# Differential attention on one Trainium2 core: half of the probability tiles take VectorE and DRAM instead of TensorE's transpose

## The chip, the cores and the metric

The kernel runs on one core of a Trainium2 chip. A core has TensorE (PE, matrix products and transposes through an identity), VectorE (DVE), ScalarE (ACT) and GpSimd (POOL), which run side by side and wait for each other through semaphores; here every DMA is issued from SyncE's queue (SP). The metric is device microseconds of one execution. The kernel before has a median of 1415.15 us over three runs (1411.51 to 1417.58); its profiled execution took 1413.83 us, of which 1412.0 us lie between the first and the last instruction (the span).

## The reference: what is computed

A trunk of two layers over 1024 tokens of width 1024. Each layer normalizes its input, modulates it by vectors made from a condition, runs an attention branch with a SiLU gate and adds the projected result to the residual. Layer 0 is differential attention: eight heads, each with two sets of 64-wide queries and keys and one 128-wide value.

```python
sc = einsum('bqhcd,bkhcd->bhcqk', qb, k) * scale      # c = 0, 1: two score maps a head
p = softmax(sc, axis=-1)
p = p[:, :, 0] - lam * p[:, :, 1]
o = einsum('bhqk,bkhd->bqhd', p, v)
o = rmsnorm(o, subln_g) * (1 - lambda_init)
o = o.reshape(b, s, DA_WIDTH) * silu(z)
```

Layer 1 is multi-head latent attention with one score map a head. The change lies in layer 0.

## The kernel before, in words

**Precision.** Operands are float32 numbers split into a high part, rounded to the format that TensorE multiplies, and a low remainder; each product is three matmuls, high by high, high by low and low by high (`mm3`, lines L203 to L205). A tensor that comes out of PSUM is thus copied on ACT (the high part) and subtracted on DVE or POOL (the low part).

**Layer 0's attention.** `attn0` (L1145) handles a head as four pairs of query tiles, `qp` 0 to 3, each of two tiles of 128 queries, `t` 0 and 1: eight slots a head, counted through all heads by `now[0]`. `q_tile` (L895) makes one tile: four matmuls for the score map c=0 into a PSUM buffer of 128x1024, a maximum on DVE (L433) and an exponential on ACT (L436) into an SBUF tile `e`; then the same for c=1, whose exponential stays in PSUM; a reciprocal and a scaling (L911, L912) and one DVE instruction (L913) that combines both into `e`. PSUM holds two score buffers, so map c=0 of a tile takes the buffer that the previous tile's c=0 left, and map c=1 takes the one that the previous tile's L913 has read last.

**The transpose.** P times V needs the tile with the keys on the partitions. `transpose_p` (L409) does half a tile, `kh` 0 or 1: four PE transposes of 128x128 into one PSUM buffer (L414), the high copy on ACT (L416), the low part on DVE (L419). A `Tail` (L1006) is a tile on this way: its first half is turned in the next slot, behind that slot's second score map, its second half one slot later, between that slot's two score maps. `settle` (L1093) puts the pair's products with V (`pv`, 24 matmuls with 256 columns) into the slot after the one that follows its second tile. The two pairs of a half head add into one PSUM buffer; when both are in, `close` reads it on ACT (`head_out`, L976 and L977), `subln` normalizes it with a small sum on PE in the next slot (`ssq`, L990), and `finish` (L942) spreads the row factors through DRAM, scales on POOL, splits, and stores to DRAM for the output projection.

**What fills TensorE between.** A second stream of work, the projections of the next heads (a strip for k, one for q, one for the gate, 16 steps each, a step being one `mm3` with 512 columns, product `acc`), is dealt out in steps between the pieces of a slot. `FILL0` (L41) says how many steps go into each of a slot's six places: behind score map 0, behind the second half-tile of the older tail, behind score map 1, behind the first half-tile of the newer tail, and behind each half of `pv`. Its sum over eight slots is 47. Each step also ticks a side queue, which runs the rest of a projected strip a few steps later: rotary embedding on POOL and DVE with a swap of partitions by DMA, then `stack_k` or `stack_q` (L372), which splits on ACT and POOL; `stack_q` then copies both parts to the other half of the partitions by DMA (`swap`, L384).

**The order of the instructions.** A planner orders the program at build time: on each engine it takes what its cost model finds ready, by priority in the order of the code. Three devices hold it: `pin` ties a PE instruction behind the PE instruction written before it, while `pinned[0]` is set; `behind(engine)` ties to the last marked instruction of an engine, held in `mk`; `in_turn` does for POOL what `pin` does for PE. In layer 0 `pinned[0]` is not set. In layer 1's attention it is.

**Layer 1 already has the other way.** There a pair with even `qp` is a `Mate` (L1037) and not two `Tail`s. `move` transposes the tile on DVE in blocks of 32x32 (L1047) into `eT` and stores it to DRAM (L1048). Two slots after the pair's second tile `fetch` loads both tiles from DRAM in four DMAs whose addressing moves the blocks to their place (L1054, tile `pr`). `high` (slot +4) makes the high parts on ACT (L1065), `low` (slot +5) the low parts on DVE (L1084), and the products with V come at slot +6. No PE transposes are left for that pair. The exponential that comes after `high` in the code is tied behind `high`'s copies on ACT.

Of the kernel before, what the change touches and what calls it, by code (L numbers as in the profile page):

```python
# [40 lines left out]
FILL0 = ((1, 2, 1, 1, 1, 0), (1, 1, 1, 1, 1, 1)) * 3 + ((1, 2, 1, 1, 1, 0), (1, 1, 1, 1, 1, 0))  # L41
# [57 lines left out]
def trunk(ctx: ExitStack, tc: tile.TileContext, A, out):  # L99
# [325 lines left out]
    def alloc_pt(ap_):  # L425
        pth = [ap_.tile([P, 4, 2 * P], F32R, name="pth", tag="pt", bufs=8 if ap_ is not a0b else 6) for _ in range(2)]
        ptl = [ap_.tile([P, 4, 2 * P], F32R, name="ptl", tag="pt", bufs=8 if ap_ is not a0b else 6) for _ in range(2)]
        return pth, ptl

    def softmax_part(ap_, s_ps, zs, bufs=3):  # L430

        nm = sm.tile([P, 1], F32, name="nm")
        mk["V"] = V.reduce_max(nm, s_ps, axis=AX.X, negate=True).ins  # L433
        e = ap_.tile([P, T], F32, name="e", tag="e", bufs=bufs) if ap_ else s_ps
        with tc.issue_after(mk.pop("H")) if "H" in mk else nullcontext():
            ex = S.activation(e, s_ps, AF.Exp, bias=nm, scale=1.0, accum_out=zs)  # L436
            pin_last(ex)
            mk["S"] = ex.ins
        return e
# [455 lines left out]
    def q_tile(h, half, ti, zz, ep, mid=lambda i: None):  # L895
# [5 lines left out]
        for c in range(2):  # L901
            s_ps = bank("sc", "s", [P, T])
            for src, fst in ((qa, True), (qb, False)):
                for kc in range(2):
                    PE.matmul(s_ps[:, kc * HF : (kc + 1) * HF], src[:, c, ql], KS[h][kc][:, c, :], start=fst, stop=not fst)  # L905
# [7 lines left out]
        combined.append(V.scalar_tensor_tensor(out=e0, in0=e1, scalar=z1[:, 0:1], in1=e0, op0=ALU.mult, op1=ALU.add).ins)  # L913
        return e0
# [27 lines left out]
    def finish(o, y, l, h, half, dst, ap_, dgs):  # L942

        if dst is None:
# [92 lines left out]
    class Mate(Tail):  # L1037
# [36 lines left out]
        def low(self, eng=V):  # L1074
# [18 lines left out]
    def settle(e, tail, mate, t, qp, ctx_, late):  # L1093
# [16 lines left out]
        elif t and not (late and qp == 3):  # L1110
            due.setdefault(n + (3 if late and qp == 0 else 2), []).extend([lambda: tail.pv(0), lambda: tail.pv(1)])
# [33 lines left out]
    def attn0(h, fills, extra=None, late=None):  # L1145
# [51 lines left out]

    for h in range(NH - 1):
        attn0(h, lambda i: FILL0[i])
    def load_ot(dst, src):  # L1200
# [943 lines left out]
```

## Time and profile before

| | |
|---|---|
| median of three runs | 1415.15 us |
| the profiled execution | 1413.83 us, its span 1412.0 us |
| PE busy | 1374.9 us, 97% of the span |
| DVE busy | 936.7 us, 66% |
| ACT busy | 740.3 us, 52% |
| POOL busy | 610.6 us, 43% |
| mean granted TensorE clock | 0.995 |
| DMA | 230.98 MB, 53.5% of 16 engines' span |

The times are those of a hardware profiler. PE's busy time counts a matmul from its start to its modelled end, and matmuls overlap; what one costs on a full PE is the distance between starts. Layer 0's attention runs from about 148 us (its first score map) to about 684 us (its last L913), layer 1's from 971 us to about 1317 us.

### The profile page before, as it was taken

What the parts mean: (1) busy time and instruction counts of PE and PEld (TensorE: products, weight loads), DVE (VectorE), ACT (ScalarE), POOL (GpSimd) and SP (SyncE); (2) the same over time, 40 slices, a digit from 0 to 9 for tenths busy, and PEclk for the clock granted to TensorE, in tenths of its full rate; (3) what the DMA queues carried; (4) which work ended last, traced back from release to release, by engine and by line L of the source; (5) the groups of instructions that cost most, each with busy time, mean ns of one, the idle gap of its engine ahead of it and who ended that gap; (6) DMA issues with size and microseconds to landing.
All of it is one profiled execution on the core that took longest, in us unless ns stands there. A gap on an engine that the chain in (4) does not pass through costs nothing.

```text
span 1412.0 us, 20440 instructions
## 1 busy us (share of the span) xinstructions
PE 1374.9 (97%) x7254; PEld 1150.0 (81%) x7254; DVE 936.7 (66%) x1365; ACT 740.3 (52%) x1290; POOL 610.6 (43%) x484
## 2 busy tenths in 40 slices
PE   9999899999999999999999999999999999998997
PEld 7778688888888888787778878888888888887886
DVE  7756687676777767678445787346777776764455
ACT  6623366666565655566443654345555555644342
POOL 4415164646564646462563235513142432313662
PEclk9999999999999999999999999999999999999999
DMA  9877723233333232336672222448688787776663
GB/s 352 262 226 233 237 66 103 79 103 83 105 85 95 80 96 81 97 87 221 219 240 97 97 90 90 126 146 261 164 223 248 213 240 195 204 214 214 226 213 129
DMA packets 147736, 230.98 MB, mean 164 GB/s; under 512 B 19121, under 2 KB 70449, under 8 KB 147634
## 3 DMA queue, kind: packets, MB, share of 16 engines
q1 hardware_dynamic: 147634, 229.68, 53.5%
q8 instruction: 57, 0.93, 0.3%
q14 instruction: 45, 0.37, 0.1%
HBM read 145.79 MB, written 60.23 MB: 146 GB/s over the span
## 4 chain that ended last, share of the span: by engine, by line
PE 78%; DMA 7%; DVE 6%; issue 3%; ACT 3%; SPq 2%; POOL 1%; ACTq 0%; POOLq 0%; DVEq 0%
PE acc L203 9%; PE acc L205 9%; PE acc L204 9%; PE s L1831 8%; PE s L905 7%; PE tr L414 6%; PE pv L204 4%; PE pv L205 4%; PE pv L203 4%; PE oacc L204 3%; PE oacc L205 3%; PE oacc L203 3%; PE zacc L203 1%; PE zacc L205 1%; PE zacc L204 1%
## 5 line engine op out<-in xcount | busy, mean ns | idle before, releaser
L433 DVE TENSOR_REDUCE nm<-s 128x1 f32<-128x1024 f32 x192 | 234.0, 1219 | 87.8 <-PE s L905 66.6
L416 ACT CAST pth<-tr 128x512 fp32r<-128x512 f32 x200 | 117.4, 587 | 212.8 <-PE tr L414 211.9
L436 ACT ACTIVATE e<-s,nm 128x1024 f32<-128x1024 f32 x128 | 143.2, 1119 | 94.6 <-DVE nm L433 94.2
L419 DVE TENSOR_TENSOR ptl<-tr,pth 128x512 fp32r<-128x512 f32 x200 | 137.2, 686 | 75.8 <-ACT pth L416 75.7
L254 POOL TENSOR_TENSOR wl<-wraw,wh 128x512 fp32r<-128x512 f32 (+2 forms) x82 | 102.7, 1254 | 170.4 <-ACT wh L253 162.8
L203 PE MATMUL acc<-h0h,wh 128*128 128x512 f32 x360 | 151.6, 421 | 1.8 <-DVE v_hl L393 1.7
L203 PE MATMUL pv<-pth,vt 128*128 128x256 f32 x512 | 146.4, 286 | 0.0
L204 PE MATMUL pv<-ptl,vt 128*128 128x256 f32 x512 | 145.2, 284 | 0.1
L205 PE MATMUL pv<-pth,vt 128*128 128x256 f32 x512 | 144.5, 282 | 0.0
L205 PE MATMUL acc<-h0h,wl 128*128 128x512 f32 x360 | 143.3, 398 | 0.1
L204 PE MATMUL acc<-h0l,wh 128*128 128x512 f32 x360 | 142.4, 396 | 0.0
L414 PE MATMUL tr<-ident,e 128*128 128x128 f32 x800 | 120.9, 273 | 10.1 <-DVE ptl L419 10.0
L414 PEld LDWEIGHTS tr<-ident,e 128*128 128x128 f32 x800 | 96.2, 140 | 41.6 <-DVE ptl L419 16.3
L1234 POOL TENSOR_TENSOR wol<-wor,woh 128x512 fp32r<-128x512 f32 x64 | 86.6, 1372 | 77.4 <-ACT woh L1233 71.4
L204 PEld LDWEIGHTS pv<-ptl,vt 128*128 128x128 f32 x512 | 97.2, 190 | 5.1 <-DVE ptl L419 0.4
L203 PEld LDWEIGHTS pv<-pth,vt 128*128 128x128 f32 x512 | 97.0, 189 | 4.5 <-ACT pth L416 0.4
L205 PEld LDWEIGHTS pv<-pth,vt 128*128 128x128 f32 x512 | 97.6, 191 | 0.1
L905 PE MATMUL s<-ks,qa 128*128 128x512 f32 x256 | 82.7, 403 | 6.0 <-ACT e L436 3.0
L913 DVE SCALAR_TENSOR_TENSOR e<-s,z,e 128x1024 f32<-128x1024 f32 x64 | 82.1, 1283 | 2.1
L355 POOL TENSOR_TENSOR rp_sw<-rp_sw,sinT 128x512 f32<-128x512 f32 x42 | 55.3, 1316 | 62.8 <-DMA rp_sw<-rp_raw 57.6
L205 PEld LDWEIGHTS acc<-h0h,wl 128*128 128x128 f32 x360 | 68.3, 190 | 16.4 <-POOL wl L254 0.6
L905 PE MATMUL s<-ks,qb 128*128 128x512 f32 x256 | 81.1, 396 | 0.0
(632 smaller groups left out, 3442.2 us busy)
## 6 DMA issues: line engine op xcount, KB each, us to landing
ada<-in_ada_ss SPq DMA_DIRECT2D x32, 512.0 KB, 6.4
wraw<-in_w_s SPq DMA_DIRECT2D x64, 256.0 KB, 2.8
vS<-v_hl SPq DMA_DIRECT2D x32, 512.0 KB, 5.0
vt<-vS SPq DMA_DIRECT2D x32, 512.0 KB, 5.0
wor<-in_w_out SPq DMA_DIRECT2D x64, 256.0 KB, 4.2
pS<-eT SPq DMA_DIRECT2D x28, 512.0 KB, 2.9
pr<-pS SPq DMA_DIRECT2D x56, 256.0 KB, 6.2
rp_sw<-rp_raw SPq DMA_DIRECT2D x168, 64.0 KB, 2.0
```

The costliest lines, as they stand in the source:

```text
L203: pin(PE.matmul(psum, ah, bh, start=first, stop=False))
L204: pin(PE.matmul(psum, ah, bl, start=False, stop=False))
L205: mm = PE.matmul(psum, al, bh, start=False, stop=last)
L254: sub = (lo_on or (V if pair_of else G)).tensor_sub(l_[:, :n], raw[:, :n], f32v(h_[:, :n]))
L414: pin(PE.transpose(tr[:, j, :], p[:, kt * P : (kt + 1) * P], ident))
L416: cp = S.copy(pth[kh][:, :, dst], tr)
L419: mk["V"] = V.tensor_sub(ptl[kh][:, :, dst], tr, f32v(pth[kh][:, :, dst])).ins
L433: mk["V"] = V.reduce_max(nm, s_ps, axis=AX.X, negate=True).ins
L436: ex = S.activation(e, s_ps, AF.Exp, bias=nm, scale=1.0, accum_out=zs)
L905: PE.matmul(s_ps[:, kc * HF : (kc + 1) * HF], src[:, c, ql], KS[h][kc][:, c, :], start=fst, stop=not fst)
L1234: in_turn(G.tensor_sub(lo, raw, f32v(hi)))
L1831: pin(PE.matmul(s_ps[:, kc * HF : (kc + 1) * HF], lhs, rhs(kc), start=i == 0, stop=i == 4))
```

## The change: what it does

In heads 0 to 6 of layer 0 the pairs with `qp` 0 and 2 become `Mate`s, except pair 2 of head 6: 13 pairs, 26 tiles. Head 7 stays as it was. In layer 0 the `Mate`'s low part is cut: keys of the first half (`kh` 0) on DVE, of the second half on POOL.

The PE instructions of layer 0's attention, up to head 6, are pinned to the order of the code, the score maps too, which `pin` did not reach before. `FILL0` deals out its 47 steps in another pattern.

Around it: the buffers of `e` are split over two pools (the first tile of an even pair in `a0a`, the others in two buffers of `a0b`, one more tag `eT`), and the transposed pairs have 8 buffers and not 6. `stack_q`'s swap of partitions moves from where it is made to the beginning of the next slot. For heads 0 to 5 `finish` no longer issues its steps at once: the store of the row factors, their load, the scaling, the split and the two stores go to fixed later slots, and the stores are tied behind the last marked SP instruction.

```diff
-FILL0 = ((1, 2, 1, 1, 1, 0), (1, 1, 1, 1, 1, 1)) * 3 + ((1, 2, 1, 1, 1, 0), (1, 1, 1, 1, 1, 0))
+FILL0 = ((1, 1, 1, 2, 1, 1), (1, 1, 1, 1, 1, 0), (2, 1, 2, 1, 1, 0), (1, 1, 1, 1, 1, 0)) + ((1, 1, 1, 2, 1, 0), (1, 1, 1, 1, 1, 0), (2, 1, 2, 1, 1, 0), (1, 1, 1, 1, 1, 0))
...
-        pth = [ap_.tile([P, 4, 2 * P], F32R, name="pth", tag="pt", bufs=8 if ap_ is not a0b else 6) for _ in range(2)]
+        pth = [ap_.tile([P, 4, 2 * P], F32R, name="pth", tag="pt", bufs=8) for _ in range(2)]
...
-                stack_q(qa, qb, fin())
+                stack_q(qa, qb, fin(), now[0] + 1 if h else None)
...
-                    PE.matmul(s_ps[:, kc * HF : (kc + 1) * HF], src[:, c, ql], KS[h][kc][:, c, :], start=fst, stop=not fst)
+                    pin(PE.matmul(s_ps[:, kc * HF : (kc + 1) * HF], src[:, c, ql], KS[h][kc][:, c, :], start=fst, stop=not fst))
             with tc.issue_after(combined[-1]) if c == 0 and combined else nullcontext():
-                es.append(softmax_part(None if c else ep, s_ps, zs[c], 1 if ep is a0a else 3))
+                es.append(softmax_part(None if c else ep, s_ps, zs[c], 1 if ep is a0a or tag != "e" else 2, tag))
...
         combined.append(V.scalar_tensor_tensor(out=e0, in0=e1, scalar=z1[:, 0:1], in1=e0, op0=ALU.mult, op1=ALU.add).ins)
+        if mk:
+            mk["V"] = combined[-1]
         return e0
...
     def finish(o, y, l, h, half, dst, ap_, dgs):
 
+        if dst is None and l == 0 and h < NH - 2:
+            n, d_, b = now[0], dr.tile([HF], F32, name="bc_d", tag="bcd", bufs=4), []
...
+            def scale0():
+                in_turn(G.tensor_mul(t3(o), t3(o), b[0].rearrange("p (q t) -> p t q", t=4)))
+                hooks.append(split0)
...
+            for i, f in enumerate((out_, in_, scale0)):
+                prep.setdefault(n + 1 + i, []).append(f)
+            return
...
                 r, (hi, lo) = self.views(kh)
-                if eng is G and kh == 0:
+                if kh == 0 if eng is G else kh == 1 and self.c["l"] == 0:
                     in_turn(G.tensor_sub(lo, r, f32v(hi)))
...
-        ctx_ = dict(pool=a0b, vp=a0b, pt=a0b, l=0, h=h, open=lambda half: None, close=close, o_={})
+        ctx_ = dict(pool=a0b, vp=a0b, pt=a0b, l=0, h=h, open=lambda half: None, close=close, nT=1, o_={})
...
+            moved = qp % 2 == 0 and not late and (h, qp) != (NH - 2, 2)
+            mate = Mate(qp, ctx_) if moved else None
...
-                    e0 = q_tile(h, half, (qp * 2 + t) % 4, zz, a0b, mid)
+                    own = qp % 2 == t == 0
+                    e0 = q_tile(h, half, (qp * 2 + t) % 4, zz, a0a if own else a0b, mid, "e" if own or moved or qp % 2 else "eT")
+                split_ = post.pop(now[0], [])
+                while split_:
+                    split_.pop(0)()
+                if not early:
                     fill(2)
-                tail = Tail(qp, t, e0, zz, ctx_)
-                if t and not (late and qp == 3):
-                    due.setdefault(now[0] + 2, []).extend([lambda tail=tail: tail.pv(0), lambda tail=tail: tail.pv(1)])
+                tail = None if mate else Tail(qp, t, e0, zz, ctx_)
+                settle(e0, tail, mate, t, qp, ctx_, late)
...
+    pinned[0] = True
     for h in range(NH - 1):
         attn0(h, lambda i: FILL0[i])
+    pinned[0] = False
```

More of the change, by code (lines that the diff above doesn't have):

```diff
@@ L893, in trunk, with q_tile @@
     stream0.step(Z_PRE)
-    def q_tile(h, half, ti, zz, ep, mid=lambda i: None):
+    def q_tile(h, half, ti, zz, ep, mid=lambda i: None, tag="e"):
         ql = slice(ti * P, (ti + 1) * P)
@@ L942, in finish, with out_, in_, split0 @@
     def finish(o, y, l, h, half, dst, ap_, dgs):
+        if dst is None and l == 0 and h < NH - 2:
+            n, d_, b = now[0], dr.tile([HF], F32, name="bc_d", tag="bcd", bufs=4), []
+            def out_():
+                with behind("SP"):
+                    SP.dma_start(d_.rearrange("(p t) -> p t", p=P), y)
+            def in_():
+                b.append(ap_.tile([P, HF], F32, name="bc_s", tag="osq", bufs=4))
+                with behind("SP"):
+                    SP.dma_start(b[0], d_[None, :].to_broadcast([P, HF]))
+            def scale0():
+                in_turn(G.tensor_mul(t3(o), t3(o), b[0].rearrange("p (q t) -> p t q", t=4)))
+                hooks.append(split0)
+            def split0():
+                with behind("S"):
+                    S.copy(b[0].bitcast(F32R), o)
+                in_turn(G.tensor_sub(o.bitcast(F32R), o, b[0]))
+                prep.setdefault(now[0] + 2, []).append(put0)
+            def put0():
+                for i, x_ in enumerate((b[0], o)):
+                    with behind("SP"):
+                        SP.dma_start(oS[l][h, half, i], x_)
+            for i, f in enumerate((out_, in_, scale0)):
+                prep.setdefault(n + 1 + i, []).append(f)
+            return
         if dst is None:
@@ L1110, in settle @@
         elif t and not (late and qp == 3):
-            due.setdefault(n + (3 if late and qp == 0 else 2), []).extend([lambda: tail.pv(0), lambda: tail.pv(1)])
+            due.setdefault(n + (3 if late and qp == 0 and ctx_["l"] else 2), []).extend([lambda: tail.pv(0), lambda: tail.pv(1)])
     def after_scores(fill, i, between=False):
```

6 lines of the change are left out of this document (3 added, 3 removed).

## The prediction, written before the result was known

> **What bounds the kernel now.** I read the page first, for which engine ends the work.
>
> ```profile
> PE 1374.9 (97%) x7254; PEld 1150.0 (81%) x7254; DVE 936.7 (66%) x1365; ACT 740.3 (52%) x1290; POOL 610.6 (43%) x484
> ...
> PE 78%; DMA 7%; DVE 6%; issue 3%; ACT 3%; SPq 2%; POOL 1%; ACTq 0%; POOLq 0%; DVEq 0%
> ```
>
> PE is busy for 97% of the span and holds 78% of the chain that ended last. An average hides stages, so next come the busy times by stretch: the heads that the change touches (165 to 560 us, and on to 640), head 7, and layer 1's attention, which already has `Mate` pairs and a pinned PE.
>
> ```profile
> core 0: us, PE busy (x) PEld busy (x) DVE busy (x) ACT busy (x) POOL busy (x), PEclk, DMA share, GB/s
> 165.00:560.00 395.00, 394.71 (x2207) 334.88 (x2206) 286.08 (x407) 242.85 (x429) 218.20 (x181) 1.00 0.32 92
> 560.00:640.00 80.00, 77.95 (x433) 64.93 (x432) 57.39 (x81) 49.35 (x89) 44.63 (x37) 1.00 0.32 92
> 640.00:690.00 50.00, 45.10 (x273) 37.70 (x272) 36.72 (x57) 29.77 (x54) 16.92 (x16) 1.00 0.58 202
> 1000.00:1240.00 240.00, 238.94 (x1390) 206.34 (x1389) 178.89 (x219) 133.05 (x224) 79.89 (x61) 1.00 0.78 215
> ```
>
> From 165 to 560 us PE never waits (394.71 of 395), at a granted clock of 1.00, while DVE is busy for 72%, ACT 61%, POOL 55%. Time there is PE work, so PE work that goes is time that goes, as long as nothing else begins to hold PE. Layer 1 shows the same mechanism with PE at 238.94 of 240.
>
> **What a transpose costs on PE.** Busy times overlap, so the price is the distance between starts. PE's timeline in a steady slot, with start and duration as its first columns:
>
> ```profile
> 309.66 0.39 PE L205 MATMUL acc<-h0h,wl 128*128 128x512 f32 x1
> 309.89 0.60 PE L414 MATMUL tr<-ident,e 128*128 128x128 f32 x4
> 310.24 0.48 PE L203 MATMUL acc<-h0h,wh 128*128 128x512 f32 x1
> 310.56 0.40 PE L204 MATMUL acc<-h0l,wh 128*128 128x512 f32 x1
> ...
> 311.03 0.62 PE L905 MATMUL s<-ks,qa 128*128 128x512 f32 x2
> 311.49 0.61 PE L905 MATMUL s<-ks,qb 128*128 128x512 f32 x2
> 311.94 0.39 PE L203 MATMUL acc<-h0h,wh 128*128 128x512 f32 x1
> ...
> 313.77 0.28 PE L203 MATMUL pv<-pth,vt 128*128 128x256 f32 x1
> 313.89 0.28 PE L204 MATMUL pv<-ptl,vt 128*128 128x256 f32 x1
> ```
>
> A projection matmul starts 0.23 us after the one ahead (309.66 to 309.89), so a step of three is 0.69. From the first of four transposes to the second matmul behind them it is 310.56 - 309.89 = 0.67; less that one matmul's 0.23, four transposes cost 0.44. A score map is 311.94 - 311.03 = 0.91, a pair's product 24 x 0.12 = 2.88.
>
> Removed are 26 tiles x 2 groups of four = 52 groups: 52 x 0.44 = **22.9 us** of PE. The modelled ends would say 0.60 a group (31.2 us in all), and the 0.35 to the next start alone 18.2; I take the distance between starts with the neighbour's delay, and keep the others as bounds. `FILL0` still deals out 47 steps a head, so the same matmuls remain otherwise.
>
> **What lands on the other engines, a half head of four slots.** A half head takes now 8 score maps (7.28), 23.5 steps (16.2), 8 groups (3.5), 2 products (5.8) and the small sum, some 33.5 us; the change makes it 33.5 - 4 x 0.44 = 31.7. The rows that price the rest, first what goes (page, costliest groups), then what comes (layer 1's tiles, min/median/max in ns):
>
> ```profile
> L416 ACT CAST pth<-tr 128x512 fp32r<-128x512 f32 x200 | 117.4, 587 | 212.8 <-PE tr L414 211.9
> L419 DVE TENSOR_TENSOR ptl<-tr,pth 128x512 fp32r<-128x512 f32 x200 | 137.2, 686 | 75.8 <-ACT pth L416 75.7
> ```
> ```profile
> L1047 DVE STREAM_TRANSPOSE eT<-e x28: 1232/1245/1248, 979.2 to 1251.7; 128x1024 f32<-128x1024 f32 x28
> ...
> L1054 SPq DMA_DIRECT2D pr<-pS x56: 318/450/1511, 987.6 to 1260.1; - x56
> L1065 ACT CAST pth<-pr x28: 1035/1043/1057, 996.4 to 1273.3; 128x1024 fp32r<-128x1024 f32 x28
> L1084 DVE TENSOR_TENSOR ptl<-pr,pth x27: 1214/1217/1777, 1000.4 to 1275.1; 128x1024 fp32r<-128x1024 f32 x27
> L1081 POOL TENSOR_TENSOR ptl<-pr,pth x1: 2349/2349/2349, 1273.5 to 1273.5; 128x1024 fp32r<-128x1024 f32 x1
> ...
> DMA to landing us min/median/max: 3.4/6.2/11.4
> ```
>
> DVE: minus 4 x 0.686, plus 2 x 1.245 and 1.217: +0.96, to 24.3 + 1.0 = 25.3 of 31.7 us (80%). ACT: minus 4 x 0.587, plus 2 x 1.043: -0.26. POOL: +2.35, to 18.5 + 2.35 = 20.9 (66%). DMA: 2 MB a pair more, 66 GB/s beside 92; layer 1 moves 215 with PE full. SP: two stores and four loads more, about 2.5 us of issue. No engine becomes the bound in the mean, so these cost nothing while PE covers them.
>
> The Trainium skill speaks against this change: VectorE: DVE Perf Modes, section Rules for kernel authors, says to use TensorE for a 128x128 transpose where PSUM will do as its destination, and DVE's only for 32x32. By busy time alone it is right here: 1.245 us on DVE, and a trip through DRAM, for 0.88 on PE. By that rule the tile stays on PE and nothing is won; the trace's stretch says that DVE has the time and PE hasn't.
>
> **Waits in the new order, slot by slot.** Map c=1 of a slot waits for L913 of the slot before. Between two maps c=1, PE has (places of `FILL0`): slot 0 to 1, 0.91 + 5 steps + a group + 0.91 + 2 steps + a group = 7.5; 1 to 2 and 3 to 0, with a product between, over 8; slot 2 to 3, 0.91 + 4 steps + 0.91 + 2 steps = **5.96**. The chain that must fit in, from the timeline:
>
> ```profile
> 303.93 0.62 PE L905 MATMUL s<-ks,qa 128*128 128x512 f32 x2
> ...
> 305.05 1.22 DVE L433 TENSOR_REDUCE nm<-s 128x1 f32<-128x1024 f32 x1 [1.01 <-PE s L905]
> ...
> 306.29 0.59 ACT L416 CAST pth<-tr 128x512 fp32r<-128x512 f32 x1
> ...
> 306.76 1.11 ACT L436 ACTIVATE s<-s,nm 128x1024 f32<-128x1024 f32 x1
> ...
> 307.77 0.21 ACT L436 ACTIVATION_READ_ACCUMULATOR s<-s,nm 128x1 f32 x1
> ...
> 308.63 0.16 DVE L911 RECIPROCAL z<-z 128x1 f32<-128x1 f32 x1
> ...
> 309.14 1.29 DVE L913 SCALAR_TENSOR_TENSOR e<-s,z,e 128x1024 f32<-128x1024 f32 x1
> ```
>
> It took 310.43 - 303.93 = 6.5 us, of which about 0.45 were the exponential behind a transposed half's copy and 0.65 the reciprocal behind four small DVE instructions: 5.4 undisturbed. In slot 2 no tail is turned, so no such copy is in the way. The wait there is thus between 0 and 0.54 us, 13 times: 0 to 7 us; I take **2**, nearer to the undisturbed row. Behind a held score map everything on PE waits, since it is pinned.
>
> Head 6 is a special place: its pair 0 is multiplied one slot later than in other heads, its unmoved pair 2 earlier, and both use the one `pv` buffer. The second half's product must wait until pair 0's is in and read. The reading costs
>
> ```profile
> L977 ACT ACTIVATE o<-pv,g 128x512 f32<-128x512 f32 x15 | 10.2, 683 | 0.0
> L976 ACT ACTIVATE osq<-pv 128x512 f32<-128x512 f32 x15 | 9.0, 598 | 22.1 <-PE pv L205 22.1
> ```
>
> 1.3 us, some 1.5 with hand-overs, once: **+1.5** (0 if the planner finds other work, 3 at most). The moved swap and the spaced `finish` I cost at nothing: the second half's queries are wanted four slots later, the stores only by the output projection; head 7's first queries are swapped at the start of the very slot that uses them, and since SP runs ahead of PE that is hidden too, or costs their 2.5 us once.
>
> SP gets a new wait: the store of `eT` stands for DVE's transpose, and behind it on SP are the weight strips and the partition swaps of the rotary step, for which POOL waits. Layer 1 shows how long:
>
> ```profile
> SPq L1048 <- DVE eT L1047: 111.4, 26, 7.5
> ```
>
> 4.3 us a wait, 7.5 at most, and there PE stayed full. A strip is fetched 16 steps, over 20 us, ahead of its split, so it covers any such wait; a swap has four steps, some 4 us, and one that comes 3 us late lets POOL stand 3 us of the 10.8 it has free in a half head. Without that cover DVE's rotary addition, and then the maxima behind it, come as late as the swap. I cost it at nothing.
>
> **Sum:** 1413.83 - 22.9 + 2 + 1.5 = **1394.4 us**, made against the profiled execution; the median of the runs stands 1.3 above that execution, which the range takes in. Bounds: with 31.2 and no wait 1382.6, with 18.2, 7 and 3 it is 1405.6.
>
> **The rivals.** (a) *The tight slot eats the gain.* In slot 2 DVE also has the moved pair's low part (1.22) ahead of the next map's maximum. If the chain stays at 6.5 and that lies in it, 13 x (0.54 + 1.22) = 22.9 comes back: 1413.83 - 22.9 + 22.9 + 1.5 = 1415, no change. Against it: the maximum that it delays belongs to map c=0, which has a slot with a product after it (over 8 us) to catch up.
>
> (b) *DVE and POOL hold each other; slower.* The low part is now cut between them, both reading SBUF, released by the same ACT copies.
>
> ```profile
> L993 DVE TENSOR_TENSOR sl_f<-zz x16: 152/653/1265, 181.8 to 681.5; 128x4 f32<-128x4 f32 x16
> ```
>
> Four elements take 152 ns or up to 1265, which looks like standing behind one POOL instruction. Held for POOL's 2.35 in the tight slot, with the tight slot's own 0.54 and 1.22 not caught up, a half head loses 4.1: 13 x 4.1 = 53, and 1413.83 - 22.9 + 1.5 + 53 = 1445; half as often, 1419. It decides from about 2.5 us a half head on, beyond what the slot with the product gives back. Against it: L1084's median beside layer 1's POOL is 1217, its worst 1777.
> The Trainium skill, SBUF — State Buffer, section Who interferes with whom, states this as a rule: a DVE instruction with two SBUF inputs and a POOL instruction that reads SBUF share a read port, and the later one fully blocks. L993's spread agrees; by that rule the low part on DVE waits up to the 2.35.
>
> (c) *The load comes late; slower.* SP works in order, and ACT's next exponential is tied behind `high`.
>
> ```profile
> SPq L230 <- POOL wl L254: 72.6, 35, 9.0
> ...
> SPq L444 <- POOL rq_y L998: 39.9, 12, 9.9
> ```
>
> From the load's place (start of slot 3) to its copy there are 8.6 + 7.5 + some 6.8 = 22.9 us. The longest wait on SP (9.9), four issues (1.8) and the slowest landing (11.4) make 23.1, which just fits; two such waits in a row make it 10 us late, and on four of the 13 pairs that gives 1394.4 + 40 = 1434.
>
> (d) *The planner doesn't do what the code says:* PE already ran the written order in the steady slots above, so pinning alone changes nothing, and no separate time follows.
>
> **How the numbers follow.** Forecast 0.78, its own range 1388 to 1405; (a) 0.12, spread from 1405 to 1417; (b) 0.06; (c) 0.04. The range 1388 to 1411 holds the forecast but for a thin tail and half of (a), about 0.8. A measurement of this kernel tells about 0.5% (7 us) from no change: faster means under 1408. Faster 0.79 (the forecast, and a little of (a) for its own tail), same 0.12, slower 0.09.
>
> **What would show it.** Right: 592 transposes (800 - 208), 54 DVE transposes, 148 of L416, and between the first score map and head 7 a PE busy share over 98%, with waits of PE on L913 under 5 us in all. Score maps waiting on L913 by 15 us or more, once a half head, would be (a); L1084 with a mean near 2 us or more beside such waits would be (b); ACT's L1065 waiting on `pr` would be (c). The price of a group would be wrong if PE stays full and the stage shrinks by something else than 23 us. The forecast is wrong above 1408.

## The result, and the profile after

The changed kernel has a median of 1483.83 us (four runs, 1478.98 to 1487.41) beside 1416.22 us of the kernel before on the same chip: ratio **1.0481**, 95% interval 1.0440 to 1.0523. It is 68 us slower; the forecast was 1394.4 us. Its profiled execution has a span of 1477.2 us and a mean granted clock of 0.971. Below, 1% is 14.15 us.

Line numbers moved: scores are still L905, softmax L433 and L436; `Mate.move` is L1079 and L1080, `fetch` L1086, `high` L1097, the low part L1113 on POOL and L1116 on DVE, the head's end L1008, L1009 and L1015, its small sum L1022 to L1030, the new path of `finish` L951 to L971. From the page of the changed kernel, the engines, the chain by engine, and three rows with counts:

```profile
PE 1371.7 (93%) x7046; PEld 1143.5 (77%) x7046; DVE 959.8 (65%) x1352; ACT 737.1 (50%) x1264; POOL 649.4 (44%) x497
...
PE 67%; DMA 10%; DVE 9%; POOL 5%; issue 4%; ACT 4%; SPq 1%; POOLq 0%; ACTq 0%; DVEq 0%
...
L416 ACT CAST pth<-tr 128x512 fp32r<-128x512 f32 x148 | 86.8, 586 | 149.1 <-PE tr L414 148.6
...
L414 PE MATMUL tr<-ident,e 128*128 128x128 f32 x592 | 92.3, 279 | 12.4 <-DVE ptl L419 12.3
...
pr<-pS SPq DMA_DIRECT2D x108, 256.0 KB, 5.8
```

The change does what it says: 592 transposes, 148 copies of half tiles, 108 loads. PE lost 208 instructions and only 3 us of busy time, and its share of the chain fell from 78% to 67%: other engines and DMAs now end PE's waits. The busy times by stretch, columns as in the prediction, say where:

```profile
165.00:560.00 395.00, 349.37 (x1809) 293.37 (x1810) 275.35 (x354) 214.26 (x364) 221.08 (x166) 0.94 0.52 138
560.00:640.00 80.00, 62.83 (x299) 52.03 (x298) 48.26 (x61) 35.81 (x60) 41.88 (x33) 0.87 0.39 111
...
1060.00:1300.00 240.00, 238.12 (x1382) 205.25 (x1381) 176.37 (x215) 132.72 (x222) 77.02 (x60) 1.00 0.76 209
```

From 165 to 560 us PE is busy for 349.4 of 395 us, where it was never idle, and the granted clock is 0.94; that is 88%, where the prediction's sign of being right was over 98%. Layer 1's attention runs as before. So nearly the whole loss lies in layer 0's attention: 63 of the 65 us by which the span grew, as the next view shows. The same view over that stage alone, from 147 us to the start of its last L913, of before and then of after:

```profile
147.00:684.00 537.00, 525.01 (x2917) 442.48 (x2916) 389.90 (x562) 323.96 (x573) 279.66 (x232) 0.99 0.37 109
```
```profile
147.00:747.00 600.00, 520.81 (x2703) 434.94 (x2702) 414.96 (x545) 320.33 (x546) 320.74 (x245) 0.93 0.51 140
```

PE's idle time went from 12.0 to 79.2 us. Its busy time fell by 4.2 and not by 22.9: if the price of the transposes holds, matmuls were made longer by 18.7 us in all, which goes with the lower granted clock (0.93 for 0.99). Together -22.9 + 67.2 + 18.7 = +63.0, the 63 us by which the stage is longer; the 18.7 is what is left over, so the sum has to come out. PE's waits of the changed kernel (total, times, longest, in us) name what ends the idle time:

```profile
PE s L905 <- DMA qa<-qa: 44.9, 6, 8.1
PE tr L414 <- DVE ptl L419: 12.3, 10, 3.3
PE acc L205 <- POOL wl L254: 10.9, 6, 5.3
...
PE s L905 <- DVE e L913: 4.1, 3, 2.6
```

Six waits of over 7 us for `qa`, the queries, at the first score map of heads 1 to 6. Before, the longest wait of all on PE was 3.7 us. One of the six on PE's timeline (start, duration, idle time ahead):

```profile
212.52 0.28 PE L205 MATMUL pv<-pth,vt 128*128 128x256 f32 x1
220.02 1.19 PE L905 MATMUL s<-ks,qa 128*128 128x512 f32 x2 [7.21 <-DMA qa<-qa]
221.01 1.21 PE L905 MATMUL s<-ks,qb 128*128 128x512 f32 x2
222.01 0.63 PE L203 MATMUL acc<-h0h,wh 128*128 128x512 f32 x1
...
224.56 0.40 PE L204 MATMUL acc<-h0l,wh 128*128 128x512 f32 x1
```

PE stands for 7.21 us, and the map behind the gap takes 222.01 - 220.02 = 1.99 us for 0.91. What the DMA waited for shows on POOL and on SP:

```profile
208.70 2.40 POOL L1113 TENSOR_TENSOR ptl<-pr,pth 128x1024 fp32r<-128x1024 f32 x1
```
```profile
211.12 1.81 SPq L1086 DMA_DIRECT2D pr<-pS  x4
213.05 1.16 SPq L384 DMA_DIRECT2D qa<-qa  x2
214.29 1.19 SPq L384 DMA_DIRECT2D qb<-qb  x2
```

The load of the next pair (L1086) fills the one buffer `pr`, which POOL's half of the last pair's low part reads until 211.10. SP works in order and stands at this load. In heads 0 to 5 the load of pair 2 and the swap of the next head's first queries (L384) are both put at the beginning of the head's last slot, the swap behind the load; here it leaves at 213.05 to 215.5 and lands behind 1 MB of load. The transfer itself became slow too, before and then after (us, minimum, median, maximum over all swaps):

```profile
DMA to landing us min/median/max: 2.2/2.6/8.0
```
```profile
DMA to landing us min/median/max: 2.2/6.1/7.0
```

### The profile page after: what moved, and what is told of

Read it like the earlier page. It is cut to its first block, busy times and chain, and to the rows that moved or that the text cites. A ratio compares the mean times of both kernels' runs of the same rounds, so it can differ in the third digit from the quotient of the medians.

```text
span 1477.2 us, 20197 instructions
## 1 busy us (share of the span) xinstructions
PE 1371.7 (93%) x7046; PEld 1143.5 (77%) x7046; DVE 959.8 (65%) x1352; ACT 737.1 (50%) x1264; POOL 649.4 (44%) x497
## 4 chain that ended last, share of the span: by engine, by line
PE 67%; DMA 10%; DVE 9%; POOL 5%; issue 4%; ACT 4%; SPq 1%; POOLq 0%; ACTq 0%; DVEq 0%
PE s L1871 9%; PE acc L205 7%; PE acc L203 7%; PE acc L204 7%; PE s L905 6%; PE tr L414 4%; PE pv L203 3%; PE pv L204 3%; PE pv L205 3%; DMA qa<-qa 3%; PE oacc L203 3%; PE oacc L205 3%; PE oacc L204 3%; POOL wl L254 1%; PE zacc L203 1%
## 5 line engine op out<-in xcount | busy, mean ns | idle before, releaser
L433 DVE TENSOR_REDUCE nm<-s 128x1 f32<-128x1024 f32 x192 | 232.9, 1217 | 103.7 <-PE s L905 81.2
L436 ACT ACTIVATE e<-s,nm 128x1024 f32<-128x1024 f32 x128 | 143.1, 1118 | 173.0 <-DVE nm L433 172.8
L254 POOL TENSOR_TENSOR wl<-wraw,wh 128x512 fp32r<-128x512 f32 (+2 forms) x82 | 108.1, 1321 | 164.1 <-ACT wh L253 152.0
L416 ACT CAST pth<-tr 128x512 fp32r<-128x512 f32 x148 | 86.8, 586 | 149.1 <-PE tr L414 148.6
L419 DVE TENSOR_TENSOR ptl<-tr,pth 128x512 fp32r<-128x512 f32 x148 | 101.5, 686 | 71.6 <-ACT pth L416 71.4
L905 PE MATMUL s<-ks,qa 128*128 128x512 f32 x256 | 86.1, 418 | 51.6 <-DMA qa<-qa 44.9
L414 PE MATMUL tr<-ident,e 128*128 128x128 f32 x592 | 92.3, 279 | 12.4 <-DVE ptl L419 12.3
L414 PEld LDWEIGHTS tr<-ident,e 128*128 128x128 f32 x592 | 73.4, 144 | 37.3 <-DVE ptl L419 16.9
L905 PEld LDWEIGHTS s<-ks,qa 128*128 128x128 f32 x256 | 46.1, 197 | 62.6 <-issue 36.1
L436 ACT ACTIVATE s<-s,nm 128x1024 f32<-128x1024 f32 x64 | 69.9, 1092 | 37.4 <-DVE nm L433 37.3
L905 PE MATMUL s<-ks,qb 128*128 128x512 f32 x256 | 84.6, 412 | 0.0
```

What stands on the lines that cost most here:

```text
L254: sub = (lo_on or (V if pair_of else G)).tensor_sub(l_[:, :n], raw[:, :n], f32v(h_[:, :n]))
L414: pin(PE.transpose(tr[:, j, :], p[:, kt * P : (kt + 1) * P], ident))
L416: cp = S.copy(pth[kh][:, :, dst], tr)
L419: mk["V"] = V.tensor_sub(ptl[kh][:, :, dst], tr, f32v(pth[kh][:, :, dst])).ins
L905: pin(PE.matmul(s_ps[:, kc * HF : (kc + 1) * HF], src[:, c, ql], KS[h][kc][:, c, :], start=fst, stop=not fst))
```

## The experiments

The theory from this trace: the swap behind the load costs most of the loss. Its rivals: the pinned order costs it, since on a pinned PE everything waits behind a late piece; the low part costs it, on DVE through the tight chain or on POOL by its length, each holding the other; the new path of `finish` and the new order of the steps cost it. The expectations stand as they were written, with names that these theories had then.

**The swap.** e1 puts the swap ahead of the load in the same slot; e2 issues it where it is made, as before the change.

```diff
-            prep.setdefault(slot, []).append(swap)
+            prep.setdefault(slot, []).insert(0, swap)
```


> The changed kernel with one thing moved: the swap of the query partitions stands ahead of the load of the transposed pair in SP's queue of its slot, and no longer behind it. Theory A (the load waits on SP for POOL's half of the low part, and the swap behind it comes late and also lands late): the six waits of 7.0 to 8.1 us at the head starts (44.9 us) go nearly all, and with them the half-clock stretches behind each, some 2 us of matmul time apiece; 1483.8 - 45 - 13 = 1426, between 1418 and 1436. Theory B (POOL with its 2.35 us more per pair is late as a whole, the swap is only where it shows): the wait moves to the next thing that POOL makes, the low parts of weights and of the queries; the gain is under 20 us, 1465 or more.


```diff
-                stack_q(qa, qb, fin(), now[0] + 1 if h else None)
+                stack_q(qa, qb, fin())
```


> The changed kernel with the swap of the query partitions issued where it is made, as before the change, not in the next slot. Theory A: as with the swap ahead of the load, 1418 to 1436, and within 5 us of that run, since both put the half that is wanted first ahead of the load. Theory B: 1465 or more.

e1: 1451.37 us, ratio 1.0256 (1.0233 to 1.0280). e2: 1446.15 us, 1.0204 (1.0165 to 1.0242). Against the changed kernel e2 wins 2.8% of the time before, 39 us (31 to 47, from the two intervals). Both runs lie above theory A's 1418 to 1436 and below theory B's 1465. The stage and two rows of PE's waits, of e2:

```profile
147.00:715.00 568.00, 519.08 (x2707) 432.72 (x2706) 420.33 (x546) 320.40 (x546) 323.08 (x245) 0.96 0.53 148
```
```profile
PE acc L205 <- POOL wl L254: 16.7, 10, 5.3
...
PE s L905 <- DMA qa<-qa: 6.4, 4, 3.5
```

The wait for the queries fell from 44.9 to 6.4 us (10.5 in e1), the swap's median landing from 6.1 us to 2.4 (2.6 in e1), and the stage is 32 us shorter in the profiled executions. It is the largest part, and it is not all: 2% remain. What follows starts from e2.

**No pair moved, and the pin.** e3 keeps everything but moves no pair (V's second load comes two slots earlier, as the `Tail`s need it). e9 also has the old `FILL0`, the old `finish` and the swap at its old place, and e17 also leaves PE unpinned; e4 is the changed kernel, unpinned.

```diff
-            prep.setdefault(n + (2 if late else 4), []).insert(0, lambda: load(1))
+            prep.setdefault(n + (2 if late or not mate else 4), []).insert(0, lambda: load(1))
-            moved = qp % 2 == 0 and not late and (h, qp) != (NH - 2, 2)
+            moved = False
```


> The pinned order, the new dealing-out of steps, the deferred swap and the spaced output steps, but no pair moved: all pairs of layer 0 go over TensorE's transpose again (the load of the second half of V comes two slots earlier, since the first pair is multiplied earlier). Theory A: no load stands ahead of the swap, so no wait at the head starts; near the kernel before, 1410 to 1425. Theory C (pinning and the other dealing-out cost by themselves): 1430 or more, with waits of TensorE on the combining instruction or on the transposes' copies.

> No pair moved, the swap issued where it is made, the steps dealt out and the output steps as before the change: what is left of the change is the pinned TensorE order in layer 0 and the other buffers. My prediction said that pinning alone changes nothing, since TensorE already ran the written order: then 1413 to 1418. The run with no pair moved lost 15.5 us; if it is the pinning that lost them, 1422 to 1430, with waits of TensorE on the transposes' copies; the rest of it would be the new pattern and the fixed slots.


```diff
-    pinned[0] = True
     for h in range(NH - 1):
         attn0(h, lambda i: FILL0[i])
```


> The changed kernel without the pinning of TensorE in layer 0's heads 0 to 6. Theory A: the swap is as late as ever and the score map still waits for it; the planner can put a few projection steps ahead, so 1455 to 1485 with the waits at the head starts still there. Theory C: 1395 to 1420, with those waits gone.

> As e9 (no pair moved, old steps, old finish, swap at its old place), but PE is not pinned in layer 0 either: what is left of the change are the buffers (two of `e` and one more pool, eight transposed pairs), the earlier load of V and where new work is placed in the code. If pinning is what costs e9 its 0.9%, this runs as before, 1.000 within 0.003, and the waits of the transposes L414 on L419 fall from e9's 15.3 us in 18 places to before's 10 in 9. If the buffers or the placing cost it, it stays at 1.007 to 1.011, some 10 us above before.

e3: 1429.40 us, 1.0104 (1.0072 to 1.0136). e9: 1425.04 us, 1.0088 (1.0068 to 1.0108). e17: 1413.71 us, 0.9997 (0.9983 to 1.0012). The stage in e17 and in e9:

```profile
147.00:686.00 539.00, 526.29 (x2921) 442.54 (x2919) 390.82 (x561) 324.27 (x572) 279.39 (x232) 0.99 0.37 109
```
```profile
147.00:696.00 549.00, 526.15 (x2915) 441.64 (x2914) 390.91 (x560) 324.44 (x572) 279.92 (x232) 0.99 0.36 107
```

The work is the same (526.3 and 526.2 us), the idle time 12.7 and 22.9. So the buffers cost nothing, and the pin costs 0.9%, 13 us (9 to 16), with no pair moved at all. e3, with the new steps, the new `finish` and the moved swap besides, is not to be told from e9: without a moved pair those cost nothing that is clear of the noise. PE's waits in e17 and in e9 show the kind of place:

```profile
PE tr L414 <- DVE ptl L419: 11.4, 11, 3.3
PE s L905 <- DVE e L913: 2.6, 3, 0.9
```
```profile
PE tr L414 <- DVE ptl L419: 15.3, 18, 3.3
PE s L905 <- DVE e L913: 5.7, 6, 2.6
```

Transposes that wait for their PSUM buffer (L419 reads it last), and maps for L913: short waits, at which an unpinned PE has a step of a projection placed ahead. With the pairs moved it is the other way round: e4 took 1492.24 us, 1.0548 (1.0515 to 1.0581), slower than the pinned kernel by 0.7% (0.1 to 1.2), although its PE never waits for `qa`; its waits for `wl` L254 alone are 31.4 us in 13 places. Neither theory expected this. The order that the planner finds for the moved pairs is worse than the written one. No run leaves e2 unpinned, so what the pin costs beside moved pairs and an early swap is not known.

**The low part.** All start from e2. e11 leaves the moved pairs' low part out, e13 POOL's half of it, e14 DVE's half; the products use the high part in its place. e5 does it all on DVE. e15 does it one slot earlier.

```diff
+            if self.c["l"] == 0:
+                self.pt = self.pt[0], self.pt[0]
...
-            if eng is V and self.done:
+            if eng is V and self.done or self.c["l"] == 0:
```


> As the run with the swap issued where it is made (1446.2 us), with the low part of the moved pairs left out: the products use the high part twice, so VectorE has 1.22 us and GpSimd 2.35 us less a pair and the two never meet there. If the low part, by its time or by the shared holding of VectorE and GpSimd, makes the remaining waits, 1400 to 1420. If the waits come from the order in which the engines' queues are bound to each other, 1432 to 1448.


```diff
-            for kh in range(2):
+            for kh in (0,) if self.c["l"] == 0 else range(2):
```


> As the run with the swap issued where it is made (1446.2 us), with GpSimd's half of the low part left out (the products use the high part there); VectorE's half stays. Without any low part it was 1417.8. If it is GpSimd's 2.5 us in its in-order queue that make the 28 us: 1415 to 1425. If it is VectorE's half in the tight slot: 1440 to 1447. If it is the two holding each other, each half alone gives most of it.


```diff
-            for kh in range(2):
+            for kh in (1,) if self.c["l"] == 0 else range(2):
```


> As the run with the swap issued where it is made (1446.2 us), with VectorE's half of the low part left out; GpSimd's half stays. If VectorE's half (1.2 us by itself, 1.57 here) in the tight slot makes the 28 us: 1415 to 1425. If it is GpSimd's half: 1440 to 1447. If it is the two holding each other, 1415 to 1430 in this run as in the other.


```diff
-                if kh == 0 if eng is G else kh == 1 and self.c["l"] == 0:
+                if eng is G and kh == 0:
```


> As the run with the swap issued where it is made (1446.2 us), and the low part of the moved pairs wholly on VectorE, as in layer 1: VectorE gets 1.22 us more a pair, GpSimd 2.35 us less, and the pair's buffer comes free earlier. Theory D (GpSimd is the engine that is late: its half of the low part stands ahead of weight splits and rotary steps): the waits on the weights' low part (15.6 us) and on the queries' swap (6.4) fall by more than half, with the half-clock stretches behind them; 1418 to 1434. Theory E (GpSimd is not loaded but held, by waiting in order for the small sums of the output scaling, which come late from VectorE and TensorE): those waits stay, 1440 to 1455.


```diff
-                post.setdefault(n + SPLIT_AT + 1, []).append(mate.low)
+                post.setdefault(n + SPLIT_AT + ctx_["l"], []).append(mate.low)
```


> As the run with the swap issued where it is made (1446.2 us), with the whole low part written one slot earlier, behind the high part, in a slot that has a product and is over 8 us long, not in the tight slot of 5.96 us between its second score maps. If the tight slot is what makes the low part dear (my rival a): 1420 to 1432. If it costs as much in any slot, since the queues are bound in order: 1438 to 1450.

| | ratio to before, 95% | against e2 |
|---|---|---|
| e11, no low part | 1.0031 (1.0010 to 1.0052) | -24 us (-31 to -18) |
| e14, none on DVE | 1.0073 (1.0047 to 1.0098) | -19 us (-25 to -12) |
| e13, none on POOL | 1.0145 (1.0119 to 1.0172) | -8 us (-15 to -2) |
| e15, one slot earlier | 1.0171 (1.0148 to 1.0194) | -5 us (-11 to +2) |
| e5, all on DVE | 1.0276 (1.0248 to 1.0304) | +10 us (+3 to +17) |

The stage in e11:

```profile
147.00:688.00 541.00, 508.85 (x2702) 426.42 (x2701) 391.71 (x532) 319.80 (x546) 279.21 (x232) 0.97 0.55 155
```

The low part is worth 24 us, most of it by DVE's half, and giving DVE the other half too makes it worse: POOL's load by itself is not the cause, and theory D falls (in e5 PE's waits for `wl` in the stage are 19.2 us, where e2 has 15.6). Even without it e11 is no faster than before: its PE work is 16 us less (508.85 against 525.01), its idle time 20 us more (32.2 against 12.0).

How the low part reaches PE shows in e2 at head 6's first map; DVE, then POOL, then PE:

```profile
561.05 2.24 DVE L1116 TENSOR_TENSOR ptl<-pr,pth 128x1024 fp32r<-128x1024 f32 x1
...
566.83 1.76 DVE L359 TENSOR_TENSOR rp_r<-rp_r,rp_sw 128x512 f32<-128x512 f32 x1 [2.40 <-POOL rp_sw L355]
```
```profile
560.91 1.30 POOL L254 TENSOR_TENSOR wl<-wraw,wh 128x512 fp32r<-128x512 f32 x1
562.16 3.38 POOL L1113 TENSOR_TENSOR ptl<-pr,pth 128x1024 fp32r<-128x1024 f32 x1
565.50 1.29 POOL L355 TENSOR_TENSOR rp_sw<-rp_sw,sinT 128x512 f32<-128x512 f32 x1
566.75 1.29 POOL L254 TENSOR_TENSOR wl<-wraw,wh 128x512 fp32r<-128x512 f32 x1
...
569.31 1.25 POOL L377 TENSOR_TENSOR qb<-rp_r,qa 64x512 fp32r<-64x512 f32 x1 [1.27 <-ACT qa L375]
```
```profile
571.63 1.19 PE L905 MATMUL s<-ks,qa 128*128 128x512 f32 x2 [3.53 <-DMA qa<-qa]
```

DVE's half takes 2.24 us where the prediction's row had 1.217: it began while POOL's split of a weight strip (L254) ran. POOL's half began while DVE's ran and takes 3.38 (its median in the changed kernel's trace is 2.40). The rotary multiplication L355 stands behind POOL's half, DVE stands 2.40 us for it and then needs 1.76 for its sum, beside the next weight split, and the split and the swap that follow bring the queries 3.53 us late. The groups of L359 in layer 0 of before, the changed kernel, e11, e14 and e13 (count, busy, mean ns), with DVE's half of the low part in the changed kernel (L1116) and in e13 (L1118):

```profile
L359 DVE TENSOR_TENSOR rp_r<-rp_r,rp_sw 128x512 f32<-128x512 f32 x28 | 22.3, 796 | 3.0 <-POOL rp_sw L355 2.8
```
```profile
L359 DVE TENSOR_TENSOR rp_r<-rp_r,rp_sw 128x512 f32<-128x512 f32 x28 | 31.0, 1105 | 15.3 <-POOL rp_sw L355 15.2
L1116 DVE TENSOR_TENSOR ptl<-pr,pth 128x1024 fp32r<-128x1024 f32 x13 | 23.0, 1769 | 0.0
```
```profile
L359 DVE TENSOR_TENSOR rp_r<-rp_r,rp_sw 128x512 f32<-128x512 f32 x28 | 24.8, 887 | 12.1 <-POOL rp_sw L355 6.5 <-DMA pr<-pS 5.5
```
```profile
L359 DVE TENSOR_TENSOR rp_r<-rp_r,rp_sw 128x512 f32<-128x512 f32 x28 | 30.6, 1093 | 13.1 <-POOL rp_sw L355 12.4 <-DMA bc_d<-rq_y 0.6
```
```profile
L359 DVE TENSOR_TENSOR rp_r<-rp_r,rp_sw 128x512 f32<-128x512 f32 x28 | 29.9, 1067 | 8.2 <-POOL rp_sw L355 8.0
L1118 DVE TENSOR_TENSOR ptl<-pr,pth 128x1024 fp32r<-128x1024 f32 x13 | 21.7, 1672 | 0.0
```

With any low part in, L359 takes 1.07 to 1.11 us in these runs, without one 0.89. Against the kernel before, DVE loses 28 x 0.31 = 8.7 us in L359 of the changed kernel, and 13 x 0.55 = 7.2 in L1116, beside the 13 x 1.22 = 15.9 us of the work itself. POOL's half of the low part is not what holds them: with it left out (e13) both stay nearly as long. In the changed kernel's trace 20 of these 41 DVE instructions took longer than 0.70 and 1.22 us. All 20 began while a POOL instruction ran: POOL's half in three cases (6.0 us in all), a weight split L254 in six (6.3 us), other steps in the rest. So putting work on DVE makes it meet what POOL does anyway. That the low part costs 24 us is shown; how much of it is this holding, and how much the place of the two halves in their queues, no run separates.

**The other parts.** All start from e2 again. e6 has the old `finish`. e7 runs the small sum of a head's end (L1022 to L1030) right behind a slot's fourth fill instead of at its end, since POOL, in order, stands for its row factors; e16 is e7 and e15 together. e8 has the old `FILL0`. e12 leaves DVE's transpose out (the tile itself is stored and loaded), which frees 1.24 us of DVE a tile. e10 moves pair 2 alone, in six heads.

```diff
-        if dst is None and l == 0 and h < NH - 2:
+        if False:
```


> As the run with the swap issued where it is made (1446.2 us), with the output steps (factors through DRAM, scaling, split, stores) issued as before the change instead of in fixed later slots. Theory D and theory E: within 5 us of 1446, since the wait for the small sums comes ahead of these steps. If the fixed slots are what holds GpSimd or the DMA queue, 1415 to 1435.


```diff
         fill(i)
+        for f in new if rest_early[0] else []:
+            hooks.remove(f)
+            f()
         for j in range(max(2, len(todo_))):
...
-        for f in new:
+        for f in [] if rest_early[0] else new:
```


> As the run with the swap issued where it is made (1446.2 us), with the small sum and what hangs on it (TensorE's small matmuls, VectorE's and GpSimd's small steps) written one place earlier in its slot, behind the first half-tile's transpose and its steps, not at the slot's end. Theory E: GpSimd's waits on the small sums (73 us, longest 13) fall to half or less, the waits on the weights' low part (15.6 us) nearly go; 1418 to 1434. Theory D: within 6 us of 1446.

> The run with the low part one slot earlier, and the small sum one place earlier in its slot besides (alone 1443.2 us, with the waits on the weights' low part down from 15.6 to 8.7). If both take away what binds the remaining waits: 1405 to 1420, near the kernel before. If one wait takes the place of another, 1430 to 1445.


```diff
-FILL0 = ((1, 1, 1, 2, 1, 1), (1, 1, 1, 1, 1, 0), (2, 1, 2, 1, 1, 0), (1, 1, 1, 1, 1, 0)) + ...
+FILL0 = ((1, 2, 1, 1, 1, 0), (1, 1, 1, 1, 1, 1)) * 3 + ((1, 2, 1, 1, 1, 0), (1, 1, 1, 1, 1, 0))
```


> As the run with the swap issued where it is made (1446.2 us), with the steps dealt out as before the change (the same 47 a head). If the new pattern is fitted to the moved pairs, slots 0 and 2 lose steps that cover the chain from score map to combined tile: waits on the combining instruction grow by 5 to 15 us, 1450 to 1465. If the pattern doesn't matter, within 5 us of 1446; theory E would allow a gain, to 1430, where the weight splits come to lie ahead of the small sums.


```diff
-            mk["V"] = V.transpose(eT.rearrange("p (c k j) -> p c k j", c=4, j=32), e.rearrange("p (k c i) -> p c k i", c=4, i=32)).ins
+            if self.c["l"]:
+                mk["V"] = V.transpose(eT.rearrange("p (c k j) -> p c k j", c=4, j=32), e.rearrange("p (k c i) -> p c k i", c=4, i=32)).ins
+            else:
+                eT = e
```


> As the run with the swap issued where it is made (1446.2 us), with VectorE's transpose of the moved tiles left out: the tile itself is stored and loaded, so the DMA trip stays and VectorE has 2.5 us less a pair. If VectorE's load delays the maxima and the rotary additions, 1415 to 1432; if not, 1438 to 1450.


```diff
-            moved = qp % 2 == 0 and not late and (h, qp) != (NH - 2, 2)
+            moved = qp == 2 and not late and h != NH - 2
```


> As the run with the swap issued where it is made (1446.2 us), but only the pair 2 of heads 0 to 5 is moved: 6 pairs and not 13 (the load of the second half of V comes two slots earlier). If the loss goes with the number of moved pairs, starting from the run with none (1429.4): 1429.4 + 6/13 x 16.8 = 1437, between 1432 and 1441. If a pair costs only where it meets its neighbour half's pair, one pair a head wins its 1.76 us: 1413 to 1425.

| | median | ratio to before, 95% |
|---|---|---|
| e6, old `finish` | 1456.14 us | 1.0284 (1.0264 to 1.0305) |
| e7, small sum early | 1443.24 us | 1.0194 (1.0173 to 1.0214) |
| e16, e7 and e15 | 1452.43 us | 1.0271 (1.0247 to 1.0294) |
| e8, old `FILL0` | 1442.63 us | 1.0203 (1.0169 to 1.0237) |
| e12, no DVE transpose | 1440.99 us | 1.0201 (1.0179 to 1.0224) |
| e10, pair 2 alone | 1457.57 us | 1.0323 (1.0303 to 1.0343) |

e6: the new path of `finish` is no cause; without it e2 is 0.8% slower. e8 and e12 are not to be told from e2: neither the order of the steps nor the 32 us of DVE transposes is what limits it. e7's reason stood in e2's trace, on POOL, with the wait on PE that came of it:

```profile
539.59 1.01 POOL L180 TENSOR_TENSOR rq_y<-sl_w,mhalf 128x4 f32<-128x4 f32 x1 [12.63 <-DVE sl_w L1028]
...
544.96 1.27 POOL L254 TENSOR_TENSOR wl<-wraw,wh 128x512 fp32r<-128x512 f32 x1
```
```profile
546.28 0.80 PE L205 MATMUL acc<-h0h,wl 128*128 128x512 f32 x1 [5.30 <-POOL wl L254]
```

POOL stands 12.63 us for four numbers a partition, and the split of a weight strip behind them comes 5.3 us late for PE. With the sum early, e7's waits of PE are:

```profile
PE acc L205 <- POOL wl L254: 9.8, 7, 4.9
PE ssq L1022 <- ACT osq L1008: 6.8, 2, 6.6
```

The waits for `wl` fell from e2's 16.7 to 9.8 us, and as much came elsewhere: PE now waits 6.8 us for the square on ACT that the early sum needs. One wait took the place of another, and the time stayed, so theory E's gain (1418 to 1434) did not come either. e16 did the same at a loss. e8 did it at no change:

```profile
PE s L905 <- DVE e L913: 15.9, 17, 4.1
```

17 waits on L913 against e2's four (4.7 us): the new `FILL0` does what it is for, and its 11 us come back in other places.

e10 is slower than e2 with 6 instead of 13 pairs moved, which no theory expected. Its waits of PE name something that e2 hasn't:

```profile
PE tr L414 <- DVE ptl L419: 24.7, 24, 3.3
PE pv L203 <- ACT o L1009: 11.7, 6, 2.9
```

With pair 2 alone moved, each head hands its one `pv` buffer from one half to the other without time between, six times some 2 us; the waits of the transposes are 12 us more than e2's 12.6. That makes it no measure of the price of a pair, and I leave it so.

No version ran faster than the kernel before.

## Why the prediction was wrong

The forecast's mechanism was that PE has 22.9 us less to do and stays full. The first half held and the second didn't. Step by step, in parts of the time before (the profiled execution: forecast 0.9863):

- **"52 x 0.44 = 22.9 us of PE"**: the count is right. No run measures the price by itself. The same distance between starts, taken in the trace of the kernel before at the 80 groups between 165 and 560 us that two projection matmuls follow, is 0.44 us in the mean (0.437 to 0.495), and e11's 16.2 us less of PE work, at a granted clock of 0.97 in the place of 0.99, is not against it.
- **"The moved swap and the spaced `finish` I cost at nothing"**, **"since SP runs ahead of PE that is hidden too, or costs their 2.5 us once"**: this is the step that failed first. I looked for the queries in time at head 7 alone, and there at the issue time of the swap alone. Head 7, which has no such load ahead of its swap, is not among the six late heads. The first queries of heads 1 to 6 are swapped at the start of the slot ahead of the one that uses them, which is earlier than head 7's, but behind a load that waits for a buffer. Measured: +2.8%, 39 us (31 to 47), by e2. Of SP's new waits I had counted those for `eT`, and not the wait of the load that the change itself puts ahead of the swap.
- **"pinning alone changes nothing"** (in rival d): +0.9%, 13 us (9 to 16), by e9 and e17, with no pair moved; with the pairs moved the pinned kernel is the faster one (e4). The reason given, that PE already ran the written order in the steady slots, was read from some 4 us of one slot. A few short waits a head, which another step filled before, are enough.
- **"these cost nothing while PE covers them"**, for the busy time on DVE and POOL: the low part alone costs 1.7%, 24 us (18 to 31). Part of it is rival (b)'s mechanism, at the place I named (L1116, mean 1769 ns) and at a second one that I had not: L355 on POOL and L359 on DVE behind it, on the way to the queries. But what holds DVE is mostly not POOL's half, as (b) had it, and (b)'s sign was such a mean beside score maps that wait 15 us or more for L913, which did not come. The busy shares said that there was time; on a pinned PE, with DVE and POOL each in order, a late piece holds PE although its engine is idle elsewhere.
- **+2 and +1.5 for the tight slot and the `pv` buffer**: maps waited 4.1 us for L913, three times; two of these (0.68 and 0.85 us) lie in the tight slot, so its wait was 1.5 and near the 2. No wait of the products for the buffer's reading stands in the list of the changed kernel. With swap and low part out (e11) the moved pairs give 0.6% against e9, 8 us (4 to 12), where 19.4 were priced (e11 also has the new steps and the new `finish`); the 11 us between are not assigned to one cause. In e7 and e8 waits that fell in one place came back in another.

These add up: 0.9863 - 0.0003 (e17) + 0.0091 (pin) + 0.0080 (moved pairs without the rest) + 0.0173 (low part) + 0.0277 (swap) = 1.0481. The terms are differences of a chain of kernels, so they must add up; the order in which the parts are undone could shift their sizes, the pin's above all.

Of the rivals, (a) fell: L913 holds PE for 4.1 us and not for 15 or more. (c) looked at the right queue and the wrong victim: ACT's `high` never waits for `pr` in the list of waits, but the swap behind the load came late at six heads. (c) also called 23.1 us in a place of 22.9 a fit. (b) was the nearest, at 1445 us, with a chance of 0.06. That e2, which has no late swap, lies at 1446 is chance: (b)'s 53 us were waits for L913, and e2's loss is made of the pin, the low part and moved pairs that give less. That all three could hold at once was in none of the cases: each was priced with the others at nothing, and the range of 1388 to 1411 came from that.

## What to carry to other kernels

A DMA that is put into an in-order queue must be priced by what stands behind it: ask which buffer it waits for, who frees that buffer, and whether something urgent comes next in the same queue, then place the urgent one ahead (here one line, 39 us). An engine that is full because a planner has always other work at hand can lose that cover when its order is fixed (here 0.9%): measure the fixed order with nothing else changed first. And the busy shares of the engines that receive work do not say what the move gains: in the stage DVE was busy for 415 of 600 us and POOL for 321, and pieces that came late still held PE.

## What the runs showed of the hardware that was not expected

**Gaps of some microseconds slow what follows.** After a gap of 7.21 us a score map took 1.99 us for 0.91, and matmuls 0.63 for 0.40, until some 4.5 us later, as if TensorE ran at half its clock; the window from 560 to 640 us has a granted clock of 0.87. Over the stage this would make the 18.7 us worked out above; in e2, with 48.9 us of idle time, it is 519.08 - 502.1 = 17.0, in e11, with 32.2, 6.7. The Trainium skill, TensorE: Matmul & The Clock Gate, section Why this matters for your kernels, has a rule that gaps of more than about 3 us between bursts of matmuls put the clock back to half; the trace agrees, by those rows. Idle time alone does not do it: e9 is idle for 22.9 us of the stage, after its first 16 us in waits of at most 1.3 us, and its granted clock there stays at 0.99. The price of a gap of several microseconds in a full PE is thus more than the gap.

**DVE and POOL hold each other both ways.** A subtraction of two SBUF tiles on DVE, begun behind one on POOL, took 2.24 us for 1.22, and POOL's, begun behind that, 3.38 for 2.40. The Trainium skill, SBUF — State Buffer, section Who interferes with whom, says that a DVE instruction with two SBUF inputs and a GpSimd instruction that reads SBUF contend for a shared port, and that the order of issue decides who waits. The trace agrees: of the 41 L359 and L1116 in layer 0 of the changed kernel, the 20 that took longer did so by what was left of the POOL instruction ahead of them less 0.13 to 0.15 us, and the other 21 took 0.68 to 0.70 and 1.22 us.
